# A hybrid decoder layer with product-key experts: gate tables stored by group of eight experts, eight gathers moved, two choices of experts tied to groups of tokens

## The chip, the cores and the metric

The kernel runs on one core of a Trainium2 chip. It uses TensorE (PE, matrix products), VectorE (DVE), ScalarE (ACT), GpSimd (POOL, here the indirect transfers: gathers by row and scatters) and SyncE (SP, which issues most of the plain transfers). The metric is device time in microseconds (us) of one execution; lower is better.

## The reference, cut to what matters

512 tokens and 16 learned ones pass through two branches (a diagonal state-space model and an mLSTM), are merged by gates, and then through a mixer of experts, in which all that follows happens:

```python
def block(xb):                                   # xb: tokens x 1024
    q = (xb @ w_q).reshape(-1, 8, 2, 128)        # 8 heads, two halves
    s = einsum('thid,hikd->thik', q, keys)       # 128 keys for each half
    sv, si = top_k(s, 16)
    cand = sv[..., 0, :, None] + sv[..., 1, None, :]
    cidx = si[..., 0, :, None] * 128 + si[..., 1, None, :]
    cs, ci = top_k(cand.reshape(..., 256), 16)   # the choice of 16 experts a head
    eidx = take_along_axis(cidx, ci)             # of 16384 experts
    gate = softmax(cs)
    act = gelu(einsum('td,thkd->thk', xb, u_tab[eidx]))
    return einsum('thk,thkd->td', gate * act, v_tab[eidx])
```

The output is the last RMS norm of h plus this mixer, without the 16 learned tokens. All is float32.

## The kernel before, in words

Tokens stand in four tiles of 128 (0 to 3). For tiles 1 to 3 but for the last 32 tokens of tile 3 (352 tokens), the kernel does not gather chosen experts: it forms the hidden value of every expert for every token, and multiplies it by a gate that is zero where the expert was not chosen. Experts stand in 128 blocks j of 128. For a block, `hidden` makes three matrix products of split float32 numbers for each of 8 slices of 128 (24 matmuls of 128x352, drawn as h<-x2h,uh and the like; `uh` by ScalarE and `ul` by VectorE are the high and the low part of a block of U, line 82 and 83). Tile 0 is done by gathering: 128 rows of U and 128 of V, one for each place of choice, by GpSimd (line 1143), each used in one VectorE instruction (1150 for U, 1158 for V). The last 32 tokens of tile 3 gather U as "side rows" (32 gathers, line 1366, used on line 1374).

The part after the query projections is in two stages. In the *preparation* `scores` and `pairs_of` find the chosen experts of each tile (VectorE); `pairs_of` is a generator of 13 steps for a whole tile. `gates(i, others, blocks)` then turns the choices of tile i into a dense table of gates, 32 tokens ("a block of tokens") at a time, in groups of eight: VectorE makes one-hot tables (`o`, and `ow` that is multiplied by the gate), TensorE multiplies them (gp<-ow,o, line 1505), ScalarE copies the result to `stg` (line 1507), and SP stores `stg` to the DRAM tensor `gd` (line 1513). Nine blocks of tokens go this way; three more of tile 1 are added up in another DRAM tensor, `gds`, by scatters from GpSimd (line 1425). After each group `gates` takes two steps of `others`, the choices that still have to be made (`more`: tile 2, then tile 0), and `fill` puts passes of `hidden` between. `beside` issues side rows and, once the choice of tile 0 is made, the first NEARLY rows of tile 0; it works by a planned clock (PACE us between gathers). What hidden makes here is put by in DRAM (`ad`).

In the *main loop* over j, the table of gates for eight experts at a time is read back (`gin`: gds on line 1652, gd on line 1656), multiplied by the activations (`w`, line 1660), split (`wh`, `wl`), and 18 matmuls of 128x512 add block j of V to the output of three tiles (o<-vh,wh and the like). The rest of `hidden` and the gathers of tile 0 run along; `upto` spreads the gathers evenly over the loop.

The order of instructions on each engine comes from a scheduler that plays the program through with a planned time for each; calls of `keep_in_program_order` and manual dependencies (`add_manual_dep`) fix parts of it. Each engine executes its own list in order and waits on semaphores. All SP transfers share one queue, all GpSimd transfers another. On a buffer's second use its new writer waits for its last reader.

## Time and profile before

| | us |
|---|---|
| median of 3 runs | 1655.53 |
| lowest and highest of them | 1654.82, 1656.39 |
| the profiled execution | 1656.81 |
| its span, first to last instruction | 1655.1 |
| preparation, first gp matmul to first o matmul | 685.8 to 943.7 |
| main loop, first to last o matmul | 943.7 to 1643.8 |

Granted clock of TensorE: 0.996. The views that the prediction quotes are: the page's lines on engines, groups and transfers; busy time of each engine by stage ("PE, PEld, DVE, ACT, POOL", then the clock, the transfer engines' share and GB/s); who waited for whom ("us in total, times, longest us"); the timeline (start, duration, engine, line, operation, and in brackets the idle time before and what ended it); and the chain of waits.

### The profile page before, as it was taken

Reading aid. Unit: us, or ns where it says so; the run is one execution under the profiler, and the core shown is the slowest. Engines: PE = TensorE matmul, PEld = TensorE weight load, DVE = VectorE, ACT = ScalarE, POOL = GpSimd, SP = SyncE. Lnnn points to the kernel's source line nnn. Section 1 sums busy time; section 2 is a strip of 40 time slices with the busy share of each in tenths; the row PEclk is TensorE's granted clock in tenths of the full one; section 3 lists DMA queues with packets and bytes.
Section 4 is the critical chain, followed back from the end, with each engine's and each line's share of the span. In section 5 each row is a group of like instructions: output and inputs, shape, how many; then the busy total and the mean of one; then the engine's idle time right before and its main releaser. Section 6 shows DMA issues by size and latency. Waiting matters only on the chain.

```text
span 1655.1 us, 25605 instructions
## 1 busy us (share of the span) xinstructions
PE 1619.0 (98%) x9551; PEld 1427.8 (86%) x9551; DVE 1319.5 (80%) x2639; ACT 709.8 (43%) x1159; POOL 696.4 (42%) x474
## 2 busy tenths in 40 slices
PE   7999999999999999999999999999999999999997
PEld 7898787777888899999999888888888888888885
DVE  6997643366478999999886496988888989898985
ACT  4453545423333244575664543434333334333334
POOL 2000022223122476877875253444444645565630
PEclk9999999999999999999999999999999999999999
DMA  4514253213463246789999899999999999999983
GB/s 181 129 53 97 91 176 121 65 39 102 166 219 98 74 118 191 245 298 349 310 356 341 332 362 347 378 399 369 382 357 402 378 400 376 377 398 358 379 295 119
DMA packets 147957, 423.20 MB, mean 256 GB/s; under 512 B 38228, under 2 KB 56788, under 8 KB 138360
## 3 DMA queue, kind: packets, MB, share of 16 engines
q1 hardware_dynamic: 86184, 263.00, 44.3%
q0 software_dynamic: 55360, 151.07, 25.8%
q10 hardware_dynamic: 6288, 7.49, 1.4%
q8 instruction: 75, 1.23, 0.3%
q14 instruction: 50, 0.41, 0.1%
HBM read 376.13 MB, written 45.38 MB: 255 GB/s over the span
## 4 chain that ended last, share of the span: by engine, by line
PE 84%; DVE 9%; DMA 4%; issue 1%; ACT 1%; ACTq 0%; SPq 0%; DVEq 0%
PE o L90 9%; PE o L89 9%; PE o L86 9%; PE h L90 9%; PE h L86 8%; PE h L89 8%; DMA v<-in_v 2%; PE gp L1505 2%; PE q L89 1%; PE q L86 1%; PE q L90 1%; DVE ul L83 1%; PE s L877 1%; PE n L886 1%; DVE g L1150 1%
## 5 line engine op out<-in xcount | busy, mean ns | idle before, releaser
L86 PE MATMUL h<-x2h,uh 128*128 128x352 f32 x1024 | 333.3, 325 | 1.4 <-ACT act L1106 1.0
L90 PE MATMUL h<-x2h,ul 128*128 128x352 f32 x1024 | 331.3, 324 | 1.6 <-DVE ul L83 1.4
L89 PE MATMUL h<-x2l,uh 128*128 128x352 f32 x1024 | 330.9, 323 | 0.0
L86 PE MATMUL o<-vh,wh 128*128 128x512 f32 x768 | 279.1, 391 | 3.1 <-ACT wh L1668 3.1
L89 PE MATMUL o<-vl,wh 128*128 128x512 f32 x768 | 278.7, 390 | 0.1
L90 PE MATMUL o<-vh,wl 128*128 128x512 f32 x768 | 270.5, 391 | 0.9 <-DVE wl L1684 0.8
L1143 POOL DMA_INDIRECT g<-in_v,e x128 | 191.2, 1494 | 155.7 <-DVE ac L1158 131.2
L1143 POOL DMA_INDIRECT g<-in_u,e x120 | 140.9, 1174 | 214.6 <-DVE g L1150 185.5
L82 ACT ACTIVATE uh<-u 128x1024 fp32r<-128x1024 f32 x128 | 134.7, 1060 | 210.2 <-PE h L89 189.2
L1425 POOL DMA_INDIRECT gds<-cw,ix x96 | 192.9, 2009 | 52.2 <-issue 25.9
L86 PEld LDWEIGHTS h<-x2h,uh 128*128 128x128 f32 x1024 | 193.1, 189 | 6.6 <-ACT act L1106 2.1
L90 PEld LDWEIGHTS h<-x2h,ul 128*128 128x128 f32 x1024 | 192.4, 188 | 4.6 <-DVE ul L83 2.7
L89 PEld LDWEIGHTS h<-x2l,uh 128*128 128x128 f32 x1024 | 192.5, 188 | 1.8
L83 DVE TENSOR_TENSOR vl<-v,vh 128x1024 fp32r<-128x1024 f32 x128 | 155.9, 1218 | 40.6 <-ACT vh L82 40.4
L82 ACT ACTIVATE vh<-v 128x1024 fp32r<-128x1024 f32 x128 | 135.0, 1055 | 105.0 <-PE o L90 69.7
L83 DVE TENSOR_TENSOR ul<-u,uh 128x1024 fp32r<-128x1024 f32 x128 | 155.0, 1215 | 23.0 <-ACT uh L82 22.8
L90 PEld LDWEIGHTS o<-vh,wl 128*128 128x128 f32 x768 | 144.1, 188 | 33.5 <-DVE wl L1684 3.1
L86 PEld LDWEIGHTS o<-vh,wh 128*128 128x128 f32 x768 | 143.6, 188 | 31.3 <-ACT wh L1668 4.1
L89 PEld LDWEIGHTS o<-vl,wh 128*128 128x128 f32 x768 | 143.6, 188 | 28.6 <-DVE vl L83 0.4
L1158 DVE SCALAR_TENSOR_TENSOR ac<-g,w,ac 128x1024 f32<-128x1024 f32 x127 | 162.3, 1278 | 0.8
L1150 DVE SCALAR_TENSOR_TENSOR g<-g,x 128x1024 f32<-128x1024 f32 x120 | 144.4, 1215 | 0.0
L1668 ACT ACTIVATE wh<-w 128x384 fp32r<-128x384 f32 x128 | 67.1, 524 | 175.0 <-DVE w L1660 174.1
(554 smaller groups left out, 3019.4 us busy)
## 6 DMA issues: line engine op xcount, KB each, us to landing
u<-in_ut SPq DMA_DIRECT2D x64, 1024.0 KB, 7.6
v<-in_v SPq DMA_DIRECT2D x128, 512.0 KB, 10.1
gd<-stg SPq DMA_DIRECT2D x9, 2048.0 KB, 10.4
gi<-gd SPq DMA_DIRECT2D x16, 1152.0 KB, 17.5
ad<-act SPq DMA_DIRECT2D x38, 352.0 KB, 4.9
act<-ad SPq DMA_DIRECT2D x38, 352.0 KB, 11.5
wq<-in_w_q SPq DMA_DIRECT2D x14, 512.0 KB, 3.5
gds<-qt SPq DMA_DIRECT2D x6, 1024.0 KB, 5.2
```

What stands on the lines that cost most here:

```text
L82: pin(A.activation(hi, src, AF.Copy))
L83: return eng.tensor_tensor(lo, src, f32(hi), op=OP.subtract)
L86: i_ = PE.matmul(ps, lh, rh, start=first, stop=False)
L89: PE.matmul(ps, lh, rl, start=False, stop=False)
L90: return PE.matmul(ps, ll, rh, start=False, stop=last)
L877: PE.matmul(p[:, :w], xk[kk][:, c0:c0 + P], qt[:, kk, T - w:], start=kk == 0, stop=kk == 1)
L1143: return GP.indirect_dma_start(out=t, out_offset=None, in_=a["u"] if s_ < P else a["v"], in_offset=bass.IndirectOffsetOnAxis(ap=e0[:, c:c ...
L1150: i_ = V.scalar_tensor_tensor(g, g, 1.0, x0, op0=OP.mult, op1=OP.mult, accum_out=hsl[:, c:c + 1])
L1158: i_ = V.scalar_tensor_tensor(ac0, g, w0[:, c:c + 1], ac0, op0=OP.mult, op1=OP.add)
L1425: i_ = GP.indirect_dma_start(out=gds.rearrange("i g b j t -> (i g b j t)").unsqueeze(1), out_offset=bass.IndirectOffsetOnAxis(ap=ix[:, c:c ...
L1505: PE.matmul(p[:, t], o1[:, a_, :, b_], ow[n][:, a_, :, b_], start=n == 0, stop=n == np_ - 1)
L1668: tc.keep_in_program_order(A.activation(wh, w, AF.Copy))
```

## The change

- `gd` was laid out as [block of tokens][partition][expert][token]: a store wrote 16 KB in one run a partition, and the read for eight experts took nine runs of 1 KB. It is now [partition][group of eight experts][block of tokens][expert][token]: a store writes 16 runs of 1 KB a partition, and the read takes one run of 9216 bytes.
- NEARLY is 0 instead of 8: no row of tile 0 is gathered in the preparation. All 256 rows of tile 0 (it was 248) are gathered in the loop.
- PACE is 5.0 instead of 4.7.
- After each group of eight tokens one step of `others` is taken, not two.
- `held` wraps the choices of tiles 2 and 0: the first VectorE instruction of each step is ordered behind the last VectorE instruction that the program has written before it.

```diff
-    NEARLY = 8
+    NEARLY = 0
...
-        gd = dram.tile([NTD * P // TB - HB, P, NKEY, TB], F32, name="gd")
+        gd = dram.tile([P, NKEY // JB, NTD * P // TB - HB, JB, TB], F32, name="gd")
...
-        PACE = 4.7
+        PACE = 5.0
...
                     fill(1.25 + 0.6 * np_)
                     next(others, None)
-                    next(others, None)
-                SY.dma_start(gd[(i - 1) * (P // TB) + b - HB], stg)
+                SY.dma_start(gd[:, :, (i - 1) * (P // TB) + b - HB].rearrange("p g j t -> p g (j t)"),
+                             stg.rearrange("p (g j) t -> p g (j t)", j=JB))
...
+        def held(steps):
+
+            while True:
+                n = len(nc.cur_bb.bb.instructions)
+                if next(steps, 0) == 0:
+                    return
+                all_ = nc.cur_bb.bb.instructions
+                new = [i for i in all_[n:] if i.engine == on_v]
+                old = [i for i in all_[max(0, n - 400):n] if i.engine == on_v]
+                if new and old:
+                    tc.add_manual_dep(new[0], old[-1].name, mybir.DependencyInfo(
+                        mybir.DependencyClass.NoSync, mybir.DependencyReason.DATA), reason="order")
+                yield
+
         def more():
-            yield from filled(2)
-            yield from filled(0)
+            yield from held(filled(2))
+            yield from held(filled(0))
             placed(prs[0][1].rearrange("p h k -> p (h k)"), 0)
...
-                SY.dma_start(gin[:, HB:], gd[:, :, j:j + JB].rearrange("b i j t -> i b j t"))
+                SY.dma_start(gin[:, HB:], gd[:, j // JB])
```

The order of VectorE, before, at the last groups of the first three blocks of tokens of tile 3 (o and ow: one-hot tables; ge with hsi: uses of side rows; w, ci, sm, cf: the choice of a tile; ul: low part of a block of U):

```order
L1049 TENSOR_TENSOR o_7302<-iob,eb_6186 128x2048
L1204 MAX_INDEX ci_7005<-cs_6897,tkc_7411 128x8
L1049 TENSOR_TENSOR w_4324<-cs_6897 128x128
L1049 TENSOR_TENSOR o_7449<-iob,eb_6186 128x2048
L1049 TENSOR_TENSOR ow_7303<-o_7302,wb_6189 128x2048
L1374 SCALAR_TENSOR_TENSOR ge_6966,hsi<-ge_6966,qt_69 128x1024
L1374 SCALAR_TENSOR_TENSOR ge_7015,hsi<-ge_7015,qt_69 128x1024
L1374 SCALAR_TENSOR_TENSOR ge_7017,hsi<-ge_7017,qt_69 128x1024
L1374 SCALAR_TENSOR_TENSOR ge_7019,hsi<-ge_7019,qt_69 128x1024
L1278 CAST cf_7514<-ci_7005 128x128
L1308 TENSOR_REDUCE sm_7743<-w_4324 128x8
L1049 TENSOR_TENSOR ow_7450<-o_7449,wb_6189 128x2048
```

and the same two groups now:

```order
L1049 TENSOR_TENSOR o_6973<-iob,eb_6204 128x2048
L1309 RECIPROCAL sm_7333<-sm_7333 128x8
L1049 TENSOR_TENSOR o_7122<-iob,eb_6204 128x2048
L1049 TENSOR_TENSOR m_6936<-ge_6935,rkd_6285 128x2048
L1049 TENSOR_TENSOR m_6936<-ge_6935,rk 128x2048
L1049 TENSOR_TENSOR ow_6974<-o_6973,wb_6207 128x2048
L1374 SCALAR_TENSOR_TENSOR ge_6581,hsi<-ge_6581,qt_69 128x1024
L1374 SCALAR_TENSOR_TENSOR ge_6613,hsi<-ge_6613,qt_69 128x1024
L1049 TENSOR_TENSOR gw_6273<-gw_6273,sm_7333 128x128
L83 TENSOR_TENSOR ul_7164<-u_7161,uh_7163 128x1024
L1049 TENSOR_TENSOR ow_7123<-o_7122,wb_6207 128x2048
```

Two side rows and a split of U stand between the two ow, where four side rows and two instructions of the choice stood. Further on in the new order, at the start of tile 2's groups, there is a run of six side rows in a row between two splits of U.

The end of the preparation on VectorE, before, at the second group of the last block of tokens (ge with hsl: uses of rows of tile 0):

```order
L1049 TENSOR_TENSOR o_9199<-iob,eb_9110 128x2048
L1049 TENSOR_TENSOR ow_9200<-o_9199,wb_9113 128x2048
L1049 TENSOR_TENSOR o_9203<-o_9199,wb_9113 128x1024
L1150 SCALAR_TENSOR_TENSOR ge_8860,hsl<-ge_8860,x_68 128x1024
L1150 SCALAR_TENSOR_TENSOR ge_8862,hsl<-ge_8862,x_68 128x1024
L1150 SCALAR_TENSOR_TENSOR ge_8864,hsl<-ge_8864,x_68 128x1024
L83 TENSOR_TENSOR ul_9345<-u_9342,uh_9344 128x1024
```

and now:

```order
L1049 TENSOR_TENSOR o_9211<-iob,eb_9133 128x2048
L83 TENSOR_TENSOR ul_9420<-u_9417,uh_9419 128x1024
L1049 TENSOR_TENSOR ow_9212<-o_9211,wb_9136 128x2048
L1049 TENSOR_TENSOR o_9215<-o_9211,wb_9136 128x1024
L83 TENSOR_TENSOR ul_9451<-u_9417,uh_9450 128x1024
```

The three uses of rows of tile 0 ahead of the split are gone. Then the handoff on VectorE, from the last one-hot tables to the loop's first w, before:

```order
L1049 TENSOR_TENSOR o_9371<-o_9367,wb_9113 128x1024
L83 TENSOR_TENSOR ul_9538<-u_9504,uh_9537 128x1024
L83 TENSOR_TENSOR ul_9570<-u_9567,uh_9569 128x1024
L83 TENSOR_TENSOR ul_9601<-u_9567,uh_9600 128x1024
L83 TENSOR_TENSOR ul_9633<-u_9630,uh_9632 128x1024
L83 TENSOR_TENSOR ul_9664<-u_9630,uh_9663 128x1024
L1660 TENSOR_TENSOR w_9714<-gi_9711,act_9472 128x352
```

and now:

```order
L1049 TENSOR_TENSOR o_9341<-o_9337,wb_9136 128x1024
L83 TENSOR_TENSOR ul_9546<-u_9543,uh_9545 128x1024
L83 TENSOR_TENSOR ul_9577<-u_9543,uh_9576 128x1024
L83 TENSOR_TENSOR ul_9609<-u_9606,uh_9608 128x1024
L83 TENSOR_TENSOR ul_9640<-u_9606,uh_9639 128x1024
L1675 TENSOR_TENSOR w_9690<-gi_9687,act_9448 128x352
```

One split of U fewer stands there. On TensorE the same place has 154 U matmuls from the last gp matmul to the first o matmul before, and 128 now (128 and 154 count the last four, of the loop's own blocks).

More of the change, by code (lines that the diff above doesn't have):

```diff
@@ L1575, in more @@
             early["may"] = NSIDE + NEARLY
+        on_v = V.engine
         rest = more()
```

## The prediction

> **What bounds the kernel now.** I read the page's first and fourth parts, then busy time by stage, then who waits in the stages that the diff touches.
>
> ```profile
> PE 1619.0 (98%) x9551; PEld 1427.8 (86%) x9551; DVE 1319.5 (80%) x2639; ACT 709.8 (43%) x1159; POOL 696.4 (42%) x474
> ...
> PE 84%; DVE 9%; DMA 4%; issue 1%; ACT 1%; ACTq 0%; SPq 0%; DVEq 0%
> ```
> ```profile
> core 0: us, PE busy (x) PEld busy (x) DVE busy (x) ACT busy (x) POOL busy (x), PEclk, DMA share, GB/s
> ...
> 720.00:760.00 40.00, 38.52 (x296) 37.05 (x295) 38.74 (x63) 23.17 (x30) 34.29 (x19) 1.00 0.92 329
> 760.00:840.00 80.00, 79.59 (x602) 77.14 (x600) 75.30 (x104) 49.10 (x60) 62.96 (x37) 1.00 0.95 319
> 840.00:880.00 40.00, 39.64 (x318) 37.49 (x316) 29.46 (x33) 25.11 (x31) 30.42 (x19) 1.00 0.99 348
> 880.00:920.00 40.00, 38.56 (x298) 37.31 (x298) 28.73 (x41) 20.30 (x27) 15.86 (x10) 1.00 0.88 314
> 920.00:960.00 40.00, 38.15 (x207) 34.52 (x206) 22.24 (x31) 17.81 (x30) 11.27 (x9) 1.00 1.01 377
> ...
> 1000.00:1040.00 40.00, 38.28 (x183) 32.41 (x182) 28.07 (x45) 14.26 (x24) 13.58 (x12) 1.00 0.92 341
> 1040.00:1600.00 560.00, 559.84 (x2715) 485.32 (x2714) 502.95 (x642) 214.23 (x381) 283.32 (x207) 1.00 1.00 380
> ```
>
> TensorE sets the time, at full granted clock. The diff adds and removes no matmul, so only its idle time can change. Up to 920 us, where tables are built and U products fill in (the preparation), it idles 1.48 + 0.41 + 0.36 + 1.44 = 3.7 us; at the handoff to the main loop (920 to 960) 1.85 us; early in the loop (1000 to 1040) 1.72 us; over the next 560 us only 0.16 us. That is 7.3 us, the most that these rows let the change win, plus what overlap hides:
>
> ```profile
> 941.17 0.32 PE L90 MATMUL h<-x2h,ul 128*128 128x352 f32 x1
> 941.33 0.32 PE L86 MATMUL h<-x2h,uh 128*128 128x352 f32 x1
> ```
> ```profile
> PE o L86 <- ACT wh L1668: 2.6, 2, 1.6
> PE h L90 <- DVE ul L83: 1.4, 2, 0.8
> PE h L86 <- ACT act L1106: 1.0, 3, 0.5
> PE gp L1505 <- DVE ow L1049: 0.8, 2, 0.6
> ```
>
> A U matmul follows the last after 0.16 us and is drawn 0.32 us long, so each wait is about 0.16 us longer than the idle time shows. The waits between 700 and 1040 us are few, and those of the preparation end with VectorE (ul, ow) or behind it.
>
> **Part 1, VectorE in the preparation.** Eight gathered rows of tile 0 leave; the second and third choices come one step per eight tokens and may no longer overtake.
>
> ```profile
> L1374 DVE SCALAR_TENSOR_TENSOR ge<-ge,qt 128x1024 f32<-128x1024 f32 x32 | 37.7, 1219 | 6.9 <-DMA ge<-in_u,xsi 6.9
> ...
> L1150 DVE SCALAR_TENSOR_TENSOR ge<-ge,x 128x1024 f32<-128x1024 f32 x8 | 9.5, 1217 | 0.0
> ...
> L1374 DVE DVE_READ_ACCUMULATOR ge<-ge,qt 128x1 f32 x32 | 2.6, 81 | 0.0
> ```
> ```profile
> 732.40 1.22 DVE L1049 TENSOR_TENSOR ow<-o,wb 128x2048 f16<-128x2048 f16 x1
> 733.53 1.22 DVE L1374 SCALAR_TENSOR_TENSOR ge<-ge,qt 128x1024 f32<-128x1024 f32 x1
> ...
> 738.50 1.21 DVE L1049 TENSOR_TENSOR ow<-o,wb 128x2048 f16<-128x2048 f16 x1
> ```
>
> It loses 8 x (1.217 + 0.081) = 10.4 us of work ahead of the loop. That alone is worth nothing where VectorE has slack (840 to 920: 29 of 40 us busy), but three of the eight stood in front of a split of U at the end, the second place shown with the diff. Between 720 and 840 VectorE is busy 95%, and a group's second ow waited behind four side rows (733.5 to 738.1). In the changed order only two stand there, and fewer steps of the choices stand ahead of the groups. I count as won the idle time from 720 to 840, 1.9 us, the longest ul wait, 0.8 us, and 0.16 us each for about five of the waits listed: 3.5 us. Ends: 5 us, all the idle time of this stage with its overlap, and a loss of 2 us, since runs of six side rows stand in the new order (7.8 us, two U passes of 24 x 0.16 = 3.8 us) and could starve TensorE. The slower choices delay tile 0's e0; only the loop's gathers need it now.
>
> **Part 2, the handoff.** The last group's table goes out, is stored to gd, read back, and only then can the loop begin.
>
> ```profile
> 916.05 1.39 PE gp L1505 x24
> ```
> ```profile
> 918.99 0.33 SPq L1513 DMA_DIRECT2D gd<-stg  x1
> ...
> 931.36 4.02 SPq L1656 DMA_DIRECT2D gi<-gd  x2
> ```
> ```profile
> 941.89 1.05 ACT L82 ACTIVATE vh<-v 128x1024 fp32r<-128x1024 f32 x1
> ...
> 942.34 0.52 DVE L1660 TENSOR_TENSOR w<-gi,act 128x352 f32<-128x352 f32 x1 [10.17 <-DMA gi<-gd]
> ...
> 943.08 0.52 ACT L1668 ACTIVATE wh<-w 128x384 fp32r<-128x384 f32 x1
> ...
> 943.65 0.98 PE L86 MATMUL o<-vh,wh 128*128 128x512 f32 x3 [1.02 <-ACT wh L1668]
> ```
> ```profile
> u<-in_ut SPq DMA_DIRECT2D x64, 1024.0 KB, 7.6
> v<-in_v SPq DMA_DIRECT2D x128, 512.0 KB, 10.1
> gd<-stg SPq DMA_DIRECT2D x9, 2048.0 KB, 10.4
> gi<-gd SPq DMA_DIRECT2D x16, 1152.0 KB, 17.5
> ```
>
> From the store's issue at 918.99 to w at 942.34 are 23.35 us: 12.4 for the store (the read is issued at 931.36) and 11.0 for the read. TensorE covers it with U products; ScalarE's vh ends at 942.94, after w began, so read and cover are just in balance today. In the new order 128 U matmuls stand between the last table matmul and the first o, against 154: 26 x 0.16 = 4.2 us less cover. Store and read must now take 19.2 us, or every further microsecond is lost.
>
> The store is cut into 16 pieces of 1 KB a partition instead of one of 16 KB; the read becomes one piece of 9 KB instead of nine of 1 KB. The price of 1 KB pieces:
>
> ```profile
> 923.00:927.00 4.00, 4.00 (x27) 4.00 (x26) 1.23 (x1) 1.57 (x4) 1.99 (x2) 1.00 1.02 431
> ...
> 938.00:942.00 4.00, 3.81 (x24) 3.52 (x23) 0.00 (x0) 1.41 (x4) 0.00 (x0) 1.00 1.10 348
> ```
>
> The store with gathers beside it moved 431 GB/s (923 to 927), the reads in 1 KB pieces 348 (938 to 942). 2.1 MB at 348 instead of 431 is 1.2 us more: the store lands after 13.6. The read then resembles the load of u, 1024 KB in long pieces: 7.6. Together 21.2, so 2.0 us lost. Ends: nothing, with the store at its median of 10.4 (10.4 + 7.6 = 18.0); and 8.8 us, worked out with the second rival.
>
> The Trainium skill's "DMA: Bandwidth & Descriptors", section "Specifications", says that transfers reach line rate from 512 B up. By it the store would not slow down, this term would be 0.8 and the sum 1.2 us lower; the row at 938 us (348 against 431) disagrees, and I go by the row.
>
> **Part 3, the loop.** Two things move here. Eight gathers of 0.52 MB come in: 4.2 MB, 11.0 us of transfer at the 380 GB/s of the row from 1040 us. All sixteen reads of gd, 18.9 MB, go from 348 to at most 431 GB/s, 54.3 to 43.8 us: 10.5 us less. Together +0.5 us of transfer; +11 if 9 KB pieces gain nothing.
>
> ```profile
> L1143 POOL DMA_INDIRECT g<-in_v,e x128 | 191.2, 1494 | 155.7 <-DVE ac L1158 131.2
> ```
>
> What hides it: in the second half of the gathers alone GpSimd waits 131 us for VectorE to free a gather's buffer, so rows arrive before they are wanted; VectorE's eight further uses (10.4 us) go into 560 - 503 = 57 us of idle time there. Without that cover the eight rows cost these 10.4 us. I take nothing.
>
> What can be won is the wait for wh at 1000 to 1040.
>
> ```profile
> 986.66 22.46 DMA v<-in_v
> ...
> 1021.76 11.88 DMA gi<-gds
> ```
>
> The chain runs through a load of v that took 22.5 us (median 10.1) just behind a read of gd in 1 KB pieces on SP's queue, and then through the next gate load, which SP issues after the v loads. With long pieces that read should clear the queue in something like u's 7.6 us instead of 17.5, so v and the gate load come up to 10 us earlier. I take 1.5 of the 1.7 us; the ends are 0 and 1.9, its overlap included.
>
> **Sum.** -3.5 + 2.0 - 1.5 = -3.0 us. The profiled execution took 1656.81 us (span 1655.1, 1.7 around it) and the median of the runs is 1655.53, 1.3 below; -3.0 gives 1653.8 for the one and **1652.5** for the other.
>
> **Rivals.** *The preparation wins nothing* (new runs of side rows make the waits that the old order had elsewhere): -3.5 becomes 0, and 2.0 - 1.5 leaves 1656.0. For it: the scheduler places everything anew; against it: 10 us less VectorE work.
>
> *The store is starved at the handoff*: slower than before.
>
> ```profile
> 917.66 0.93 POOL L1143 DMA_INDIRECT g<-in_u,e  x1 [21.53 <-PE gp L1505]
> ...
> 923.44 1.86 POOL L1143 DMA_INDIRECT g<-in_u,e  x1 [0.30 <-issue]
> ```
>
> The loop's first gathers start when the last table matmul frees their buffers, beside the store: five, 2.6 MB. If small pieces take turns with the gathers' 4 KB pieces, the store ends only when all are done: 4.7 MB at 380 GB/s is 12.4 us instead of the 4.9 that its own 2.1 MB take at 431. Of today's 12.4 us of landing, 7.5 are thus latency and waiting, part of it for these same gathers; so it would land after 12.4 to 19.9, and I take 17. With the read still at 11: 28 - 19.2 = 8.8 us lost. With part 1 won and part 3 not: 1655.5 - 3.5 + 8.8 = 1660.8. It decides as soon as store and read take more than 22.7 us, where the loss outgrows part 1. The Trainium skill's "DMA: Bandwidth & Descriptors", section "Queues, rings and completion order", states this mechanism: each engine goes round its queues and drains a packet from one before it turns to the next; the gd reads' 17.5 us against 7.6 for u fit it, no row here shows a store in small pieces. Against it: the first of the five are issued before the store, and once all are through the read has the queues to itself.
>
> *The transfers bound the loop* (share 1.00): +0.5 to +11 us; with 5 in the middle and the rest as forecast but part 3's gain, 1655.5 - 3.5 + 2.0 + 5 = 1659.0. Against it: the 0.16 us of idle time in 560.
>
> *All goes well*: the cover holds and the preparation wins 5: 1655.5 - 5 - 1.9 = 1648.6.
>
> **Chances.** Forecast (1650 to 1655) 0.42; preparation wins nothing 0.20; starved store 0.17; transfers 0.06; all well 0.15. Less than 0.2% (3.3 us) can't be told from no change here. Faster by more: nearly half of the forecast and all of the last, with 0.05 for more in the loop, 0.40. Slower by more: most of the two slow rivals, 0.20. The rest, 0.40. The range reaches from just under the best case to the starved store: 1647.5 to 1661.
>
> **What would show it.** Part 1: PE idle from 720 to 920 below 1.5 us, no wait of gp for ow. Part 2: from the store's issue to the first w near 21 us; 28 proves the rival, 19 refutes my 2.0. Part 3: gi<-gd landing near 8 us, gd<-stg above 10.4; PE full from 1000 to 1040. I am wrong if TensorE's idle time moves in a stage not named, or if the loop after 1040 us shows more than 1 us of it.

## The result, and the profile after

| | before | after |
|---|---|---|
| median, us | 1655.70 (6 runs, 1654.19 to 1658.07) | 1667.59 (6 runs, 1662.59 to 1670.02) |
| ratio, 95% interval | | 1.0069 (1.0053 to 1.0084) |
| the profiled execution, us | 1656.81 | 1667.14 |
| span, us | 1655.1 | 1665.4 |
| first o matmul (loop begins), us | 943.65 | 957.05 |
| from there to the end of the span, us | 711.4 | 708.4 |

The change made the kernel slower by 0.7%: 11.9 us between the medians. 1652.5 us had been forecast. The last two rows say where: everything before the loop took 13.4 us longer, and the loop gave 3.0 us back. Busy time by stage of the kernel after, in the columns of the prediction's table:

```profile
720.00:760.00 40.00, 40.00 (x291) 39.61 (x290) 37.92 (x68) 22.55 (x28) 32.06 (x17) 1.00 0.90 290
760.00:840.00 80.00, 73.01 (x521) 70.41 (x520) 68.94 (x135) 42.29 (x52) 59.86 (x38) 0.96 0.90 299
840.00:880.00 40.00, 37.14 (x247) 35.48 (x246) 33.60 (x49) 16.76 (x24) 31.68 (x18) 0.91 0.90 268
880.00:920.00 40.00, 40.00 (x320) 39.07 (x320) 24.40 (x31) 24.59 (x30) 5.99 (x4) 1.00 0.87 294
920.00:960.00 40.00, 35.40 (x242) 33.54 (x241) 14.67 (x17) 16.99 (x25) 7.35 (x6) 1.00 0.81 304
1000.00:1040.00 40.00, 40.00 (x198) 34.91 (x197) 33.78 (x53) 15.51 (x27) 17.37 (x16) 1.00 1.02 403
1040.00:1600.00 560.00, 560.00 (x2717) 486.00 (x2716) 507.36 (x655) 216.31 (x381) 293.29 (x214) 1.00 0.99 387
```

From 760 to 880 TensorE idles 6.99 + 2.86 = 9.9 us where it idled 0.8 (0.41 + 0.36), and at the handoff 4.6 instead of 1.85. VectorE, at 75.3 of 80 us before, is busy 68.9 of 80: it waits itself. And the granted clock (the number behind POOL's busy time) is 0.96 and 0.91 where it was 1.00. What TensorE (720 to 960 us), VectorE (720 to 900) and GpSimd (660 to 760) waited for in the kernel after ("us in total, times, longest us"):

```profile
PE h L86 <- ACT act L1106: 4.5, 3, 2.7
PE h L90 <- DVE ul L83: 4.4, 2, 4.0
PE h L86 <- ACT uh L82: 3.9, 2, 2.9
```
```profile
DVE ul L83 <- ACT uh L82: 11.5, 10, 2.5
DVE ge L1374 <- DMA ge<-in_u,xsi: 8.8, 4, 4.5
```
```profile
POOL ge L1366 <- DVE ge L1374: 27.0, 3, 17.7
```

In four places VectorE stands in its fixed order before a use of a side row that has not landed. Two of them on VectorE, and GpSimd's list where it falls behind (timeline):

```profile
810.94 1.23 DVE L1374 SCALAR_TENSOR_TENSOR ge<-ge,qt 128x1024 f32<-128x1024 f32 x1 [1.98 <-DMA ge<-in_u,xsi]
...
816.66 1.23 DVE L1374 SCALAR_TENSOR_TENSOR ge<-ge,qt 128x1024 f32<-128x1024 f32 x1 [4.49 <-DMA ge<-in_u,xsi]
...
817.81 1.22 DVE L1049 TENSOR_TENSOR o<-iob,eb 128x2048 f16<-128x2048 f16 x1
818.95 1.22 DVE L83 TENSOR_TENSOR ul<-u,uh 128x1024 fp32r<-128x1024 f32 x1
```
```profile
691.06 2.25 POOL L1425 DMA_INDIRECT gds<-cw,ix  x1 [0.30 <-issue]
711.02 1.74 POOL L1366 DMA_INDIRECT ge<-in_u,xsi  x1 [17.70 <-DVE ge L1374]
...
723.07 1.68 POOL L1366 DMA_INDIRECT ge<-in_u,xsi  x1 [8.99 <-DVE ge L1374]
```

The row used at 816.66 was asked for at 805.47. Behind it stand a table and a split of U, and TensorE waits 4.0 us for that ul (the largest of its waits there). GpSimd had stood 17.7 and 9.0 us before its seventh and ninth gather, because only six rows may be in flight (NE) and the first ones, asked for from 665 on, were not used before 709.5; scatters and later gathers stood behind. The 17.7 us alone made nothing late: the seventh gather went out at 711.0 us, in the kernel before at 713.1, since GpSimd began its gathers 8.8 us earlier (665.1 against 673.9). Behind the 9.0 us they are late: the ninth went out at 723.1 us instead of 717.4, the 19th at 787.5 instead of 778.5, and the 24th, the row above, at 805.5 instead of 796.2. The uses of the 19th to the 24th row begin at 795 to 817 us, in the kernel before at 796 to 808. So these rows were asked for some 9 us later and wanted at nearly the same time.

Not all of TensorE's 9.9 us ends with a row. 4.4 us end with a ul behind a late row (0.4 at 779.5, 4.0 at 820.2). 1.0 us at 775.4 ends with uh, after a load of U that SP had issued 4.5 us behind a store and that let ScalarE go on only 13.2 us later. 1.6 us at 778.5 and 2.9 us at 851.5 end with act and uh, which stand on ScalarE behind two and three copies of tables to `stg` (from 776.2 and from 847.8 on).

A stall has a second price. TensorE behind the wait that ends at 851.5, in the kernel after:

```profile
851.53 0.66 PE L86 MATMUL h<-x2h,uh 128*128 128x352 f32 x1 [2.86 <-ACT uh L82]
...
853.52 0.49 PE L86 MATMUL h<-x2h,uh 128*128 128x352 f32 x1
853.82 0.49 PE L89 MATMUL h<-x2l,uh 128*128 128x352 f32 x1
...
858.02 0.32 PE L89 MATMUL h<-x2l,uh 128*128 128x352 f32 x1
858.18 0.32 PE L90 MATMUL h<-x2h,ul 128*128 128x352 f32 x1
```

For some 5 us the matmuls follow each other after 0.29 us instead of 0.16. Between 760 and 880 us 33 U matmuls of the kernel after start at that distance, 33 x 0.13 = 4.3 us more; the kernel before has none. PE counts as busy meanwhile, so this part is in no idle time.

The handoff on SP's queue, and ScalarE beside it:

```profile
933.43 0.53 SPq L1512 DMA_DIRECT2D gd<-stg  x1
935.54 3.06 SPq L1084 DMA_DIRECT2D u<-in_ut  x1
938.95 1.27 SPq L1667 DMA_DIRECT2D gi<-gds  x1
946.74 0.80 SPq L1671 DMA_DIRECT2D gi<-gd  x2
```
```profile
949.29 1.06 ACT L82 ACTIVATE uh<-u 128x1024 fp32r<-128x1024 f32 x1 [7.71 <-DMA u<-in_ut]
```
```profile
950.75 0.43 PE L86 MATMUL h<-x2h,uh 128*128 128x352 f32 x1 [2.72 <-ACT act L1106]
```

The read of gd is issued 13.3 us after the store, the first w begins at 953.04, 19.6 us after it. TensorE stopped before that, at 948.0, for a load of U that SP issued 2.1 us behind the store and that arrived only after 13.7 us.

### The profile page after: what moved, and what is told of

Read it like the earlier page. It is cut to its first block, busy times and chain, and to the rows that moved or that the text cites. A ratio compares the mean times of both kernels' runs of the same rounds, so it can differ in the third digit from the quotient of the medians.

```text
span 1665.4 us, 25620 instructions
## 1 busy us (share of the span) xinstructions
PE 1622.5 (97%) x9551; PEld 1433.2 (86%) x9551; DVE 1322.4 (79%) x2639; ACT 710.4 (43%) x1159; POOL 682.0 (41%) x474
## 3 DMA queue, kind: packets, MB, share of 16 engines
q8 instruction: 75, 1.23, 0.3%
## 4 chain that ended last, share of the span: by engine, by line
PE 89%; DVE 4%; DMA 4%; ACT 2%; issue 1%; ACTq 0%; DVEq 0%
PE o L90 11%; PE o L89 10%; PE o L86 10%; PE h L86 9%; PE h L90 9%; PE h L89 9%; DMA ge<-in_u,xsi 2%; PE q L86 2%; PE q L89 2%; PE q L90 2%; PE gp L1505 2%; PE s L877 1%; PE n L886 1%; PE gm L377 1%; PE gm L380 1%; PE gm L379 1%
## 5 line engine op out<-in xcount | busy, mean ns | idle before, releaser
L86 PE MATMUL o<-vh,wh 128*128 128x512 f32 x768 | 273.2, 390 | 1.5 <-ACT wh L1683 1.5
L89 PE MATMUL o<-vl,wh 128*128 128x512 f32 x768 | 273.3, 391 | 0.1
L90 PE MATMUL o<-vh,wl 128*128 128x512 f32 x768 | 265.5, 390 | 0.6 <-DVE wl L1699 0.6
L1143 POOL DMA_INDIRECT g<-in_u,e x128 | 154.9, 1210 | 236.1 <-DVE g L1150 184.6
L1425 POOL DMA_INDIRECT gds<-cw,ix x96 | 181.1, 1886 | 52.2 <-issue 25.9
L1150 DVE SCALAR_TENSOR_TENSOR g<-g,x 128x1024 f32<-128x1024 f32 x128 | 154.1, 1217 | 0.0
```

What stands on the lines that cost most here:

```text
L86: i_ = PE.matmul(ps, lh, rh, start=first, stop=False)
L89: PE.matmul(ps, lh, rl, start=False, stop=False)
L90: return PE.matmul(ps, ll, rh, start=False, stop=last)
L1143: return GP.indirect_dma_start(out=t, out_offset=None, in_=a["u"] if s_ < P else a["v"], in_offset=bass.IndirectOffsetOnAxis(ap=e0[:, c:c ...
L1150: i_ = V.scalar_tensor_tensor(g, g, 1.0, x0, op0=OP.mult, op1=OP.mult, accum_out=hsl[:, c:c + 1])
L1425: i_ = GP.indirect_dma_start(out=gds.rearrange("i g b j t -> (i g b j t)").unsqueeze(1), out_offset=bass.IndirectOffsetOnAxis(ap=ix[:, c:c ...
```

## The experiments

The theories at the start: *A*, VectorE's fixed order holds rows that have not landed, TensorE starves behind it; which of the edits does it is open (the ties, one step a group, the pace, the missing rows). *B*, the store in 1 KB pieces slows down the transfers beside it. Times of all runs, with the idle time of TensorE from 720 to 920 us and VectorE's waits for side rows from 720 to 900 in the profiled execution:

| kernel | median us | ratio to before (95%) | PE idle | row waits |
|---|---|---|---|---|
| before | 1655.5 to 1656.3 | 1 | 3.7 | 6.9 |
| after | 1667.6 | 1.0069 (1.0053 to 1.0084) | 9.9 | 8.8 |
| e1 before, new layout | 1659.2 | 1.0014 (1.0004 to 1.0024) | 7.8 | 1.0 |
| e2 after, old layout | 1663.2 | 1.0042 (1.0027 to 1.0057) | 8.2 | 6.3 |
| e3 after, no ties | 1682.1 | 1.0152 (1.0130 to 1.0174) | 24.1 | 21.7 |
| e4 after, pace 4.7 | 1658.4 | 1.0013 (1.0003 to 1.0024) | 4.3 | 0.9 |
| e5 after, rows not read | 1700.0 | 1.0259 (1.0241 to 1.0278) | 41.2 | 0 |
| e6 after, stores by ScalarE | 1665.5 | 1.0054 (1.0036 to 1.0072) | 8.5 | 7.2 |
| e7 after, old layout, pace 4.7 | 1658.2 | 1.0017 (1.0005 to 1.0028) | 7.5 | 10.2 |
| e8 before, pace 5.0 | 1663.4 | 1.0047 (1.0029 to 1.0065) | 7.9 | 6.6 |
| e9 after, uses 2 us later | 1669.1 | 1.0085 (1.0068 to 1.0102) | 10.1 | 11.6 |
| e10 before, no early rows | 1649.0 | 0.9961 (0.9949 to 0.9974) | 0.0 | 2.4 |
| e11 before, ties | 1665.6 | 1.0064 (1.0047 to 1.0081) | 4.6 | 6.0 |
| e12 before, one step | 1685.4 | 1.0178 (1.0154 to 1.0203) | 19.2 | 18.6 |
| e13 e10, old budget | 1656.9 | 1.0003 (0.9992 to 1.0014) | 3.3 | 8.2 |
| e14 e10, new layout | 1654.5 | 0.9990 (0.9981 to 0.9999) | 1.1 | 2.0 |
| e15 e10, ties | 1654.3 | 0.9991 (0.9976 to 1.0005) | 5.2 | 7.3 |
| e16 e10, one step | 1681.8 | 1.0159 (1.0142 to 1.0177) | 23.4 | 21.7 |
| e17 e10, pace 4.4 | 1649.7 | 0.9964 (0.9953 to 0.9976) | 0.1 | 4.2 |
| e18 e10, uses 4 us earlier | 1664.9 | 1.0047 (1.0031 to 1.0062) | 11.9 | 19.3 |

Idle time and waits are of one execution each; single executions of the kernel before usually lay between 1653.3 and 1660.7 us in these comparisons, so a few us of difference between two profiles is not yet a difference between two kernels. The ratios are.

### One edit undone, or the layout alone

**e1**, the layout in the kernel before (the three lines on gd of the change).

> The kernel before with the new layout of gd alone; nothing of the order in the preparation is changed by hand. Theory A (the 12 us were lost because VectorE's fixed order now holds side rows that have not landed; the layout has no part in it): PE idle time from 760 to 880 us stays near the 2 us of the kernel before, the store and the reads of the handoff take about 20 us instead of 23.4, the wait for wh at 1033 us is gone, so 1652 to 1655 us. Rival B (stores in 1 KB pieces slow down the gathers beside them in the preparation): PE idles 8 us or more from 760 to 880 us, 1660 us or more.

Slower by 0.14%, between the two expectations. Row waits stay small (1.0 us), but TensorE waits in a new place (who waited for whom, 720 to 960, e1):

```profile
PE h L86 <- ACT uh L82: 4.2, 3, 3.1
```

The 3.1 us are at 756 us: a load of U issued 0.6 us behind a store landed after 13.2 us; in the kernel before the same load, 0.4 us behind the same store, landed after 9.9 (from the trace's packets). So B has a part, by the loads of U that queue up behind a store, not by the gathers.

**e2**, the changed kernel with the old layout.

> The changed kernel with the old layout of gd, all else as changed. Theory A: the preparation loses as much as in the changed kernel (stalls of 3 to 4 us at the side rows, slow clock behind them), the wait for wh early in the loop is back and the handoff is no better: 1667 to 1671 us. Rival B: the preparation is as before, 1655 to 1658 us.

4.4 us faster than the changed kernel (1663.2 against 1667.6; the intervals just overlap), where I had expected 1667 to 1671. Most of the loss, 7 us, is there without the layout, so B alone is not the cause. At the handoff no load of U is waited for any more, though one stands 2.1 us behind the store here too. And the wait for wh at 1033 is gone without the new layout.

**e3**, without the ties.

```diff
-            yield from held(filled(2))
-            yield from held(filled(0))
+            yield from filled(2)
+            yield from filled(0)
```

> The changed kernel without the ties that hold the second and third choice in place. If these ties are what makes side rows late (A1: the scheduler may no longer fill VectorE with the choices while rows are on their way, uses come late, their buffers come free late, and GpSimd blocks for 17.7 and 9 us): stalls from 760 to 880 us fall to 2 to 4 us, 1654 to 1658 us. If it is the other edits (A2: one step a group, 5.0 us between gathers, eight rows less): 1665 us or more.

14.5 us slower still. A1 falls: in the changed kernel the ties repair something, namely one step a group (e12, e16).

**e4**, the pace.

```diff
-        PACE = 5.0
+        PACE = 4.7
```

> The changed kernel with 4.7 us between gathers as before instead of 5.0. A1: nothing moves, 1666 to 1669 us. If it is the pace (A3: rows asked for 0.3 us later each, 32 x 0.3 = 9.6 us later at the end, so that the last ones land after their place): 1655 to 1659 us.

9.2 us of the 11.9 come back: in the profiled execution, the fastest of its ten, TensorE idles 5.6 us less from 720 to 920, and the 4.3 us of half clock are gone. What VectorE still waits for rows in e4:

```profile
DVE ge L1374 <- DMA ge<-in_u,xsi: 0.9, 1, 0.9
```

In the order of the trace two things differ from the kernel after: rows 3, 5, 9, 11, 15, 22 and 28 (counted from 0) stand behind one scatter fewer on GpSimd, and rows 18 to 21, 23 and 27 to 31 are used one table (ow) later on VectorE. On the clock the gathers of rows 18 to 23 go out no earlier (788.5 to 807.7 us in e4, 787.5 to 805.5 in the kernel after); rows 19 to 21 are used 4.6 to 5.4 us later. So the slower pace does its harm here by the uses, which it brings forward. GpSimd still stands 29.3 us before the early gathers in e4: that alone doesn't cost the time. And the wait for uh at 851.5, with the half clock behind it, is not there: at this place e4 has 1.3 us for ul. It is 2.9 us, for uh, in e2 and e6, which have the pace of 5.0, and again 1.3, for ul, in e7 with 4.7. So the pace also moves work on other engines.

### Is it the rows, is it the queue

**e5**, no use reads a row.

```diff
-            pinned(V.scalar_tensor_tensor(g, g, 1.0, xrep, op0=OP.mult, op1=OP.mult,
+            pinned(V.scalar_tensor_tensor(xrep, xrep, 0.0, xrep, op0=OP.mult, op1=OP.mult,
```

> The changed kernel, but the 32 VectorE instructions that use a side row read the tile of tokens (times zero) in place of the gathered row, so they wait for no gather and no gather waits for them; the gathers are still issued. It leaves out the hidden values of the last 32 tokens of tile 3, and the scheduler moves a few splits of U between the tables, since the rows are no longer awaited in its plan either. Theory A (VectorE's fixed order waits for rows that have not landed, TensorE starves for ul, and then runs some 20 matmuls at half clock): stalls from 760 to 880 us fall from 19 us to 3 to 6 us, clock 1.00 throughout, 1652 to 1658 us. Rival (the stalls come from U loads behind the stores or from the ties, and the rows only wait along): 1663 us or more.

1700 us: a miss that says nothing on A. (The 19 us of stalls in this expectation, and the 9.5 in that of e13, are another count than the idle time in the table.) The waits for rows are gone, and another has come, 31.4 us long:

```profile
PE h L86 <- ACT uh L82: 38.2, 4, 31.4
```
```profile
754.08 0.53 SPq L1512 DMA_DIRECT2D gd<-stg  x1
794.92 2.67 SPq L1674 DMA_DIRECT2D v<-in_v  x2
797.69 0.38 SPq L1084 DMA_DIRECT2D u<-in_ut  x1
```

With no use to wait for, the scheduler moved loads of V for the loop ahead of loads of U in SP's list. The V buffers are shared with side rows (tag vraw), whose gathers had not landed on the chip; SP stood 40 us before a load that nobody needed yet, and the load of U behind it came at 797.7.

**e6**, the stores on another queue.

```diff
-                SY.dma_start(gd[:, :, (i - 1) * (P // TB) + b - HB].rearrange("p g j t -> p g (j t)"),
+                A.dma_start(gd[:, :, (i - 1) * (P // TB) + b - HB].rearrange("p g j t -> p g (j t)"),
```

> The changed kernel with the nine stores of gd issued by ScalarE on its own queue, so that no load of U stands behind a store in one queue; the order on the other engines is the same. Theory L (in 1 KB pieces a store holds the load of U that stands right behind it in SP's queue 13 us instead of 10, and this is the 2.9 us stall at 947 us): that stall falls below 1 us, the rest stays: 1663 to 1666 us. Rival (the loads are late because all transfers share the engines, whatever the queue): no change, 1666 to 1669 us.

The time is as theory L had it, 1665.5, though its interval overlaps that of the changed kernel, so the 2 us are not sure; the stage is not as theory L had it: the wait for U at the handoff is gone, and one for wh has taken its place.

```profile
PE o L86 <- ACT wh L1683: 3.8, 1, 3.8
```

From the store to the first w it now took 22.2 us instead of 19.6. The load of U behind the store let ScalarE go on after 9.9 us instead of 13.7, and the read of gd was issued 16.9 us after the store instead of 13.3: what U gains by going round the store, the store loses. Little is won by moving the store.

**e7**, old layout and pace 4.7: what is left is one step, ties, and no early row.

> Changed kernel with both undone: the old layout of gd, and 4.7 us between gathers; what is left is one step a group, the ties and no early row. Theory L: against 1658.4 us with the new layout and 4.7 us, the stall at the handoff shrinks by 2 to 3 us: 1654 to 1657 us. If the layout is neutral: 1658 us. If it helps the loop by 1.5 us as I had predicted: 1659 to 1660 us.

The same as with the new layout (1658.2 against 1658.4): the neutral case, and theory L is missed. The handoff did get better, TensorE idles 1.9 us there instead of 4.3, but row waits of 10.2 us came back in the preparation of the profiled execution; against e4's 0.9, with the same order, this shows how narrowly these rows make it or miss it.

**e8**, the pace alone.

```diff
-        PACE = 4.7
+        PACE = 5.0
```

> The kernel before with 5.0 us between gathers instead of 4.7, nothing else. In its order rows 17 to 20 are then used behind 16, 17, 18 and 18 tables where it was 19, while seven rows stand behind one scatter more. Theory P (the pace alone does the harm, since rows are asked for later and used earlier): VectorE waits for rows 5 us or more between 760 and 840 us, 1661 us or more. Rival Q (5.0 us harms only together with one step a group and the ties, which start the tables 18 us earlier): 1655 to 1658 us.

Theory P: 7.2 us slower. Rows are used in the moment they land:

```profile
798.62 1.23 DVE L1374 SCALAR_TENSOR_TENSOR ge<-ge,qt 128x1024 f32<-128x1024 f32 x1 [2.17 <-DMA ge<-in_u,xsi]
...
800.52 1.22 DVE L1374 SCALAR_TENSOR_TENSOR ge<-ge,qt 128x1024 f32<-128x1024 f32 x1 [0.67 <-DMA ge<-in_u,xsi]
...
801.67 1.22 DVE L83 TENSOR_TENSOR ul<-u,uh 128x1024 fp32r<-128x1024 f32 x1
```

Both had been asked for 14 us earlier (784.8 and 786.1). In sum VectorE waits for rows no longer than before (6.6 against 6.9 us), but in five places instead of two, and three of TensorE's waits are now 1 to 3 us long.

### The other edits alone

**e9**, the changed kernel with later uses.

```diff
-        LAG = 28.0
+        LAG = 30.0
```

> The changed kernel, 5.0 us between gathers kept, but a row's use is planned 30 us behind its gather instead of 28. In the order rows 18 to 23 are then used behind 24 tables instead of 21 to 23, and their gathers stand behind 66 to 70 scatters instead of 64 to 69. Theory P (the loss is rows that are used 8 to 11 us after they were asked for, and land after 10 to 14): VectorE's waits for rows between 760 and 840 us fall from 8.8 us to under 2, the stalls from 760 to 880 us to 4 to 8 us, 1656 to 1661 us. Rival R (5.0 us harms because the gathers themselves come later, whatever is done about the uses): 1665 us or more.

1669.1, in rival R's range, but the trace gives another reason than R. Since only six rows may be in flight, a later use also holds its buffer longer, and the next gather comes later: rows 22 to 26 were used 6 to 9 us after they were asked for, less than before the edit. Planning the use later did not make up for the lateness.

**e10**, no early rows, alone.

```diff
-    NEARLY = 8
+    NEARLY = 0
```

> The kernel before without the eight early rows of tile 0 (none instead of 8), nothing else. My prediction's Part 1 counted this as relief: 10.4 us less on VectorE, of which up to 3 us from the path: 1652 to 1655 us. Theory P: the smaller budget pulls the U products, and with them the uses of side rows, ahead of the tables (rows 18 to 20 behind 16 tables instead of 19) while the gathers stay where they were: rows late again, 1659 to 1664 us.

6.5 us faster than before, the best version but for e17, which can't be told from it, and faster than either expectation. I had expected a gain from Part 1 and a loss from theory P; P was wrong here. TensorE does not idle at all from 720 to 920 us (e10, by stage):

```profile
760.00:840.00 80.00, 80.00 (x600) 78.68 (x599) 71.80 (x99) 45.19 (x56) 63.13 (x35) 1.00 0.96 330
840.00:880.00 40.00, 40.00 (x354) 38.43 (x353) 32.48 (x31) 30.93 (x37) 31.52 (x17) 1.00 0.93 305
880.00:920.00 40.00, 40.00 (x311) 39.33 (x310) 23.49 (x31) 20.42 (x26) 7.55 (x7) 1.00 0.70 249
```

**e11**, the ties alone, in the kernel before (`held` and the two calls of it).

> The kernel before with the ties on the second and third choice alone (two steps a group, 4.7 us, eight early rows). Rows 17 to 20 are used behind 18 tables instead of 19. Theory P: nearly nothing, 1655 to 1659 us. Rival (the ties themselves hold VectorE up behind instructions that wait): 1661 us or more, with VectorE waiting at the first instruction of a step.

10.1 us slower, against theory P's "nearly nothing". GpSimd stands 36.8 us before its seventh gather, since the first six rows are used at 732 to 738 us instead of 711 to 724, and 93 U matmuls are left to cover the handoff instead of 154, where TensorE then waits 6.6 us for wh. The handoff has most of it: from 920 to 960 us TensorE idles 7.9 us instead of 1.85.

**e12**, one step a group, alone.

```diff
                     next(others, None)
-                    next(others, None)
```

> The kernel before with one step of the choices a group instead of two, and no ties. In the changed kernel the removal of the ties cost 14 us. Theory T (one step a group lets the tables start earlier and needs the ties to keep the choices from crowding ahead of rows): 1662 us or more, with stalls behind rows from 760 to 840 us. Rival (that cost came from the pace of 5.0 us as well): 1655 to 1659 us.

The dearest edit by itself, 30 us. GpSimd, then TensorE's waits for ul, and the second longest of them on its timeline, some 95 us later:

```profile
705.66 2.47 POOL L1425 DMA_INDIRECT gds<-cw,ix  x1 [0.30 <-issue]
732.46 1.74 POOL L1366 DMA_INDIRECT ge<-in_u,xsi  x1 [24.32 <-DVE ge L1374]
```
```profile
PE h L90 <- DVE ul L83: 14.8, 3, 6.8
```
```profile
828.81 0.66 PE L90 MATMUL h<-x2h,ul 128*128 128x352 f32 x1 [6.15 <-DVE ul L83]
829.27 0.49 PE L86 MATMUL h<-x2h,uh 128*128 128x352 f32 x1
```

Between them stand late rows: the seventh gather went out at 732.5 us, in the kernel before at 713.1, and the 23rd at 815.9 instead of 790.5. For this last row VectorE waited 7.6 us, until 826.4, and the ul that TensorE waits for here comes behind it.

### What the gain of e10 is, and what the rest does to it

**e13**, e10 with the budget of the fill as it was.

```diff
-        whole = 4 * 24 + 40 * 2.5 + (NSIDE + NEARLY) * 1.3 + 3
+        whole = 4 * 24 + 40 * 2.5 + (NSIDE + 8) * 1.3 + 3
```

> The kernel before without the eight early rows, but with the budget of the preparation kept at 251 (it fell to 240.6 with them), so that side rows are used behind the same tables as before and 196 U matmuls stand behind the last table matmul instead of 128. Theory E (the eight rows' time on VectorE and their gathers are what is won): stalls from 720 to 920 us at 3 to 5 us instead of 9.5, no wait for wh at the handoff, 1646 to 1651 us. Theory B (the smaller budget, which uses rows earlier and empties GpSimd's queue earlier, is what is won): 1654 to 1657 us.

1656.9, no gain: theory B of this run. Eight rows less on VectorE are worth nothing; what is won in e10 is the place of the U products. The budget says by how much planned work all of them are to be spent, and with 240.6 instead of 251 they come a little earlier between the tables and the uses of rows. Row waits in e13 are 8.2 us, in e10 2.4. Which of the changed places in e10's order wins the time was not taken apart.

**e14**, e10 with the new layout.

> The kernel before without early rows and with the new layout of gd, nothing else; beside the 1649.0 us without the layout. My prediction: +2.0 at the handoff, -1.5 in the loop (already won here without it), so 1649.5 to 1651. Theory L (a load of U right behind a store in 1 KB pieces lands after 13 us instead of 10, and TensorE waits for it at one or two places): 1651 to 1654 us. If the shorter reads help the handoff: 1646 to 1648 us.

1654.5, just above theory L's range, and my own 1649.5 to 1651 is missed: the layout costs 0.3% (the intervals 0.9949 to 0.9974 and 0.9981 to 0.9999 lie apart). The place (waits of TensorE, and ScalarE's uh, e14):

```profile
PE h L86 <- ACT act L1106: 5.7, 5, 4.4
```
```profile
935.80 1.06 ACT L82 ACTIVATE uh<-u 128x1024 fp32r<-128x1024 f32 x1 [9.37 <-DMA u<-in_ut]
```

TensorE's 4.4 us end with this load of U, issued 2.1 us behind the last store; the next 19 U matmuls follow at half clock.

**e15**, e10 with the ties.

> The kernel before without early rows and with the ties. In the order only the first twelve rows' uses move (behind 10 and 12 tables instead of 7 and 10); all later ones stay. Theory G (the late use of the first six rows keeps their six buffers, GpSimd stands before the seventh gather, and all later gathers and scatters slip): GpSimd waits 15 us or more there instead of 2.4, VectorE's waits for rows rise from 2.4 to 6 us or more, 1655 to 1662 us. Rival (the ties cost by themselves or not at all): GpSimd's wait below 8 us, and either 1649 us, or more without waits for rows.

5 us slower than e10 (0.9991 against 0.9961; the intervals 0.9976 to 1.0005 and 0.9949 to 0.9974 just don't touch). GpSimd's wait is 27.9 us, row waits 7.3: theory G in both numbers, with a time just below its range. The length of GpSimd's wait says little by itself: 27.9 us go with a loss of 5 us here, 24.3 us with one of 33 in e16. How late the gathers then go out differs: the seventh at 722.1 us here and at 732.1 in e16, against 710.1 in e10; the 19th at 790.6 and 801.3, against 780.2.

**e16**, e10 with one step.

> The kernel before without early rows and with one step of the choices a group, no ties. The first six rows are used behind 11 tables instead of 7. Theory G: GpSimd waits 20 us or more before the seventh gather, rows 12 to 20 land late, 1665 us or more. Rival (one step alone did harm only together with the early rows): 1650 to 1656 us.

Theory G: 24.3 us before the seventh gather, row waits of 21.7, 1681.8 us.

**e17** and **e18**, asking for rows earlier.

```diff
-        PACE = 4.7
+        PACE = 4.4
```

> The kernel before without early rows and with 4.4 us between gathers instead of 4.7. In the order six gathers stand one scatter earlier (rows 4, 10, 11, 16, 28 and one more), every use stays where it was. The kernel without early rows took 1649.0 us and VectorE waited 2.4 us for rows; with those waits gone at most 1 to 2 us can be won: 1647 to 1650 us. If the pace acts otherwise than through the rows' lateness: 1653 us or more.

The time is neutral and in the range, but not for the reason given: rows 18 to 21 went out at 784.5 to 788.5 us, in e10 at 780.2 to 785.3, and VectorE waited 4.2 us for rows instead of 2.4. The faster pace did not bring these rows earlier, so what earlier rows would win is not shown.

```diff
-        LAG = 28.0
+        LAG = 24.0
```

> The kernel before without early rows and with uses planned 24 us behind the gathers instead of 28. Gathers move forward in GpSimd's queue by up to six scatters (the last row stands behind 75 instead of 81), uses by up to four tables (22 instead of 26). If uses and gathers move together, the lead of a row stays at 10 to 18 us and VectorE waits little: 1647 to 1652 us. If uses overtake the gathers (a lead below 10 us at more than four rows): 1656 us or more.

15.9 us slower than e10. Uses overtook rows: 7 of the 32 came less than 10 us after the row had been asked for (4 in e10), others met landings of 11 to 14 us, and row waits are 19.3 us.

## Why the prediction was wrong, point by point

From e10 the change can be built up edit by edit, each ratio against the kernel before, in us of 1655.7: no early rows -6.5 (e10); one step and ties +9.3 (e7, +2.8 in all); pace 5.0 +4.1 (e2, +7.0); layout +4.5 (the change, +11.4). The intervals of e7 and e2, and of e2 and the change, just overlap, so each of the last two pieces is uncertain by some 3 us. In another order the pieces have other sizes (pace 5.0 costs 7.8 alone in e8, and 9.3 between e4 and the change; the layout costs 2.3 in e1, 4.8 between e10 and e14, and nothing between e7 and e4): they don't add up.

- **Part 1, the preparation: -3.5 forecast, some 10 us lost.** (The last table matmul ends at 931.9 instead of 917.4 us; 26 x 0.16 = 4.2 of these 14.4 are U products that moved ahead of it.) They are 6.2 us more idle time of TensorE from 720 to 920 and 4.3 us of half clock. This is the step that failed: "I count as won the idle time from 720 to 840". It reckoned VectorE as a sum of busy time, as if every row had landed where the order puts its use, and it did not look at ScalarE at all. Late rows end 4.4 us of the 9.9 us of idle time; 4.4 us end with act and uh behind copies of tables on ScalarE, and 1.0 with a load of U. The kernel before already showed 6.9 us of waits for rows in the very row that I quoted for the price of a use (the 6.9 at its end), and I read only its mean. Three more things were not in the sum at all: the pace of 5.0, to which I gave no price; the limit of six rows in flight, by which late uses stop GpSimd; and the clock, which made 33 matmuls slower. The risk that I did name, six side rows in a run starving TensorE, was bounded at 2 us by the length of VectorE's work; that the rows themselves could be late was not in the bound.
- **The gain I saw was there, for another reason.** Leaving out the early rows wins 6.5 us (e10), more than the 3.5 forecast, but not by the 10.4 us of VectorE that I counted: with the budget kept, the same 10.4 us are worth nothing (e13). The fill budget, which the page of the profile doesn't show and the diff changes without a line of its own, is what moved.
- **The ties and the single step.** I had read "fewer steps of the choices stand ahead of the groups" as relief. One step alone costs 30 us, the ties alone 10, both together on e10 9. In e11, e12, e15 and e16 the first six rows are used 11 to 22 us later than without the edit and GpSimd's next gathers go out later with them. With both together (e7) only the third to sixth row are used later than in e10, by 10 to 12 us, and the 19th gather is late by 9. That this lateness makes the time is shown where a wait can be followed, as in e12; how much of each loss it makes is not. In e11 most of the loss is at the handoff.
- **Part 2, the handoff: +2.0 forecast, +2.75 us of idle time measured (4.60 against 1.85), by another wait.** From store to w 21.2 us were forecast and 19.6 measured, against a cover of 19.2: by my own sign, "19 refutes my 2.0", the reason was wrong and the number came out near by luck. 2.7 us of the idle time went to a load of U behind the store, which is not in my sum. The read's issue follows the store after 13.0 to 15.2 us in all runs with the new layout and the store on SP. With the old one it is 8.7 to 9.3 us in eight runs, 10.6 in e15, 12.4 in the kernel before, 12.6 in e8 and 17.9 in e12, so the 12.4 us that I started from is one value of a wide spread. From the read's issue to w it takes 6.2 to 6.3 us in the first and 10.1 to 13.5 in the others (16.7 in e12). In sum that is 19.3 to 21.5 us with the new layout, and 19.0 to 25.6 with the old one without e12: for this path no loss is shown, for what else is in the queue there is one.
- **The rival of the starved store** had its mechanism right and its end wrong. With the transfers of all queues from the store's first packet to its last (the change, then e2 with the old layout):

```profile
q1 hardware_dynamic: 2120, 2.56, 66.6%
q0 software_dynamic: 476, 1.70, 38.7%
```
```profile
q1 hardware_dynamic: 148, 2.15, 85.8%
q0 software_dynamic: 106, 0.37, 15.1%
```

  in 11.0 us 1.70 MB of gathers went through beside the store in 1 KB pieces, in 6.0 us only 0.37 MB beside the store in 16 KB pieces. The small pieces take turns with the gathers' 4 KB pieces. The other stores of the preparation fit: with no gather beside it a store took 6.2 to 6.5 us in the kernel before (three stores) and 6.9 to 8.1 in the kernel after (three). And a piece of 1 KB took 48 to 49 ns on its engine, one of 16 KB 626 ns: 21 against 26 bytes a ns, near the 348 against 431 GB/s of my sum. The Trainium skill's "DMA: Bandwidth & Descriptors", section "Queues, rings and completion order", has the rule of turns, and these rows agree with it. The section "Specifications" of the same page of the Trainium skill puts line rate at 512 B and up; these rows do not fit that.
- **Part 3, the loop: -1.5 forecast, -3.0 measured, cause not confirmed.** The wait for wh at 1033 is gone, and TensorE is full from 960 on. But it is gone with the old layout too (e2), and one like it appears at 1124 us in e13 and at 1117 us in e17, both with the old layout; what brings it was not taken apart. Reads of gd land after 12.5 us at the median with the new layout (e6), not after 8; with the old one it is 13.6 in e7, 16.0 in e8, 17.4 in e17 and 17.5 before. From the first o matmul to the end it is 707.9 to 709.1 us in the runs with the new layout and the store on SP. With the old one it is 707.9 (e15) to 714.7 (e13), and 708.2 in e7, so the 3.0 us can't be put down to the layout.
- **The chances.** "Slower by over 0.2%" had 0.20, on rivals that sat at the handoff and in the loop. None sat where four of the five edits act: for the preparation I had a rival in which nothing is won, and none in which much is lost.

## What to carry to other kernels

Where an engine's order is fixed ahead of time, don't price an edit by the busy time it takes away, but list for each awaited transfer when it is asked for, when it lands and when it is used; a lead of 8 to 14 us on a landing of 5 to 14 us, as the side rows have here, turns into a wait when an edit moves the order by a table or two. Then do the same for the engines beside it: nearly half of the new idle time stood behind copies on ScalarE. A limit on transfers in flight ties the asking to the using, so a late use at the front can delay what follows in that queue (by some 20 us in e16 from the seventh gather to the last, by nothing at the seventh in the changed kernel, where the queue had begun earlier). Cutting a store into small pieces to make its read long can move the cost to whatever stands behind the store in its queue.

## What was unexpected of the hardware

- **The same stall may or may not bring the half clock.** In the kernel after 2.72 us of idle time between U matmuls (948.0 to 950.75) left the clock at 1.00 and the next U matmuls at 0.16 us; 2.86 us behind a run of 24 table matmuls (848.7 to 851.5) brought 16 matmuls at 0.29 us; and in e11 a gap of 1.98 us was enough, after which the clock fell only at the fifth matmul (timeline of TensorE, e11):

```profile
705.29 0.43 PE L86 MATMUL h<-x2h,uh 128*128 128x352 f32 x1 [1.98 <-ACT act L1106]
705.56 0.32 PE L89 MATMUL h<-x2l,uh 128*128 128x352 f32 x1
...
706.29 0.50 PE L90 MATMUL h<-x2h,ul 128*128 128x352 f32 x1
706.59 0.50 PE L86 MATMUL h<-x2h,uh 128*128 128x352 f32 x1
```

  The trace's record of the granted clock has the half clock in stretches of 3.41 us or twice that (779.26 to 782.67, 820.22 to 823.63 and 850.94 to 857.76 in the kernel after), and they begin 12 and 9 times 3.41 us apart. The Trainium skill's "TensorE: Matmul & The Clock Gate", in its part on the HAM clock gate, describes windows of about 3.4 us that run freely. The trace agrees: these stretches fit such a grid. Read so, where on the grid a gap falls decides whether it costs the clock; that reading is not tested by itself. The first of the three came behind gaps of 1.04 and 1.57 us (to 775.4 and to 778.5) with 16 table matmuls between; e4 has 1.23 us, 16 table matmuls and 1.57 us at the same place (to 777.0 and to 780.1), and its clock stays at 1.00 there. That gaps shorter than 3.41 us are enough is shown here; what in a stretch decides it, no run shows. In the kernel after its three episodes cost 1.2, 1.0 and 2.1 us on top of the stall (9, 8 and 16 matmuls x 0.13).
- **A load that stands right behind a store in a queue is as late as the store**: loads of U issued 0.4 to 0.6 us behind a store landed after 9.9 to 10.9 us with the old layout, and after 11.3 to 13.8 us with the new one; loads more than 20 us behind one mostly after 4.4 to 7.7 us (packets of the traces of before, after, e1, e2 and e4).
